# One small tile padded from 4 to 64 bytes, so that every weight tile lies 64 bytes further on in SBUF

## The chip, the cores and the metric

The kernel runs on one core of a Trainium2 chip. The metric is the device time of one execution in microseconds (us); less is better. Engines are named as the profile names them: PE is the matmul engine, PEld its weight load (the load of the stationary operand), DVE the vector engine, ACT the scalar engine, POOL and SP the two engines that here mostly issue DMAs.

## What is computed

Two layers of a hybrid decoder trunk, 512 tokens by 1024 features, float32. Cut to what matters:

```python
for l in range(2):
    h = rms_norm(x, gn[0])
    x = x + 0.5 * rms_norm(swiglu(h, w_ffn1_gate[l], w_ffn1_up[l], w_ffn1_down[l]), gn[1])
    h = rms_norm(x, gn[2])
    proj = h @ w_in[l]            # q, f, i, gate; attention q, k, v; two branch gates
    y_hg = hgrn2_mixer(...) @ w_branch_hgrn[l]
    y_at = swa_sink_attention(...) @ w_branch_attn[l]
    x = x + rms_norm((sigmoid(gate_a) * y_hg + sigmoid(gate_b) * y_at) @ w_out[l], gn[3])
    h = rms_norm(x, gn[4])
    x = x + 0.5 * rms_norm(swiglu(h, w_ffn2_gate[l], w_ffn2_up[l], w_ffn2_down[l]), gn[5])
```

The inner width of each SwiGLU is 2816. Nearly all arithmetic is in the products of activations with weights.

## The kernel before

Each float32 operand of a large product is split into a rounded part and a rest (`hi` and `lo`, type float32r), and a product is three matmuls: hi with hi, hi with lo, lo with hi (`mm3`, L411 to L415; every matmul is recorded at L114 in `mm`). Every matmul has its own weight load of 128x128, so PE and PEld each show 13571 instructions. A matmul is named by what it writes and reads: `acc<-s,whi` writes a PSUM tile `acc`, streams an activation tile `s` through the array and has a block of the weight tile `whi` as its stationary operand; in `acc<-whi,s` the weights stream and the activations are stationary.

The order of the matmuls is written out by hand; the other engines are scheduled around them. The SwiGLU's first half (`sevenths`, L1029, called from `fast`, L1064) is a seven-product scheme on halves of the tokens: its matmuls have 256 columns, and activations stream. The first blocks of each SwiGLU and the gates in the mixer stream 512 columns of activations (`wmm`, L417). The second half of each SwiGLU and the output projection (`down`, L699, with `piece` and `quarters`) and `project_tok` (L1016) stream 512 columns of weights over stationary activations.

Weights arrive through `Stream` (L156). `load` (L235) brings 128x1024 pieces from HBM into `w32` tiles (four slots) by DMAs on SP's queue; `split` (L322) turns each into `whi` and `wlo` (six slots each) on ACT, DVE and, for a part of them, by an accumulating DMA on POOL's queue (L360).

All SBUF tiles but the constants come from one pool, `sb`. A tag gets its slots when its first tile is asked for, one tag behind the other, and a slot's size is rounded up to 32 bytes. The first tag is `s` (`big`, L62: 61 slots of 2048 bytes, all activations), the second is `warm`, and behind it follow `w32`, `whi`, `wlo`, `tt`, `m` and the small tags. In the built program the slots of `s` start 64 bytes past a multiple of 512, and those of `w32`, `whi` and `wlo` 128 bytes past one. Blocks inside a tile are cut at multiples of 512 bytes (256-column halves at 1024), so that these two remainders hold for every large matmul's operands: counted within 512 bytes, weights lie 64 bytes, or 16 float32 numbers, behind activations.

The tile `warm` (L138) is 128x1, written once by ACT ahead of the first matmuls; nobody reads it. A second tile of the same tag is asked for in `down` (L821).

```python
def small(shape, tag, bufs=4, dt=F32):                                        # L65
    return sb.tile(shape, dt, tag=tag, name=nm(tag), bufs=bufs)
...
nc.scalar.activation(out=small([P, 1], "warm", 2), in_=eps_t, ...)            # L138
...
warm = small([P, 1], "warm", 2)                                               # L821
```

Of the kernel before, what the change touches and what calls it, by code (L numbers as in the profile page):

```python
# [10 lines left out]
AF = mybir.ActivationFunctionType  # L11
# [4 lines left out]
P = 128  # L16
# [28 lines left out]
def trunk(ctx: ExitStack, tc: tile.TileContext, xin, wall, gains, lbT, hgain, sinks, c_dist, c_mask, c_ident, out):  # L45
    nc = tc.nc
# [11 lines left out]
    def nm(s):  # L58
        seq[0] += 1
        return f"{s}_{seq[0]}"  # L60
# [4 lines left out]
    def small(shape, tag, bufs=4, dt=F32):  # L65
        return sb.tile(shape, dt, tag=tag, name=nm(tag), bufs=bufs)
# [7 lines left out]
    def const(shape, name, dt=F32):  # L74
        return cp.tile(shape, dt, tag=name, name=name)
# [59 lines left out]
    nc.vector.memset(ones, 1.0)  # L135
    eps_t = const([P, 1], "eps_t")
    nc.vector.memset(eps_t, EPS)
    nc.scalar.activation(out=small([P, 1], "warm", 2), in_=eps_t, func=AF.Copy, scale=eps_t)  # L138


    p = aux()
# [1503 lines left out]
```

## Time and profile before

| | us |
|---|---|
| median of 2 runs | 2068.94 |
| the two runs | 2067.01 and 2070.87 |
| the profiled execution | 2067.36 |
| its span, first to last instruction | 2064.8 |
| DVE busy | 1629.0 |
| ACT busy | 1249.3 |
| POOL busy | 268.0 |

The span is the time from the first to the last instruction of the profiled execution; the 2.6 us between it and that execution's time lie outside. "Busy" sums an engine's instructions, so that engines at work together are each counted in full. Starts of matmuls are recorded, their ends are modelled; the distance between two starts, called the pitch below, is therefore the better measure of PE's speed.

### The profile page before, as it was taken

How to read it: one execution, taken by the hardware profiler on the slowest of the kernel's cores; microseconds unless marked ns; L12 is line 12 of the kernel's file. 1: busy time of each engine (PE TensorE's matmuls, PEld its weight loads, DVE VectorE, ACT ScalarE, POOL GpSimd, SP SyncE). 2: the span in 40 equal slices, each digit the busy share in tenths (PEclk: the TensorE clock that was granted, in tenths of full speed). 3: DMA queues.
4: the chain of work that ended last, by engine and by line, in shares of the span. 5: the costliest groups of instructions: out<-in, count | busy, mean ns of one | idle time of the engine just before them, and what ended most of it. 6: DMA issues, size and time to landing. Idle time of an engine off the chain costs nothing. (4 is left out here: it accounts for less than half of the span.)

```text
span 2064.8 us, 36590 instructions
## 1 busy us (share of the span) xinstructions
PE 2053.1 (99%) x13571; PEld 1826.7 (88%) x13571; DVE 1629.0 (79%) x2910; ACT 1249.3 (61%) x2209; POOL 268.0 (13%) x318
## 2 busy tenths in 40 slices
PE   9999999999999999999999999999999999999999
PEld 8899978887888999997899998898778989999987
DVE  5887899666776778888988788977676758788888
ACT  7566687456355556658866666864653545666684
POOL 0111140000000011113201121400000100111140
PEclk9999999999999999999999999999999999999999
DMA  8587798312237367878758878872122562778794
GB/s 250 151 188 192 187 196 242 103 62 72 72 95 212 113 145 190 189 188 206 205 152 189 196 187 202 185 220 84 52 82 62 137 190 93 182 191 189 181 203 123
DMA packets 166802, 328.07 MB, mean 159 GB/s; under 512 B 19072, under 2 KB 85088, under 8 KB 166624
## 3 DMA queue, kind: packets, MB, share of 16 engines
q1 hardware_dynamic: 122416, 228.16, 33.1%
q0 software_dynamic: 44064, 97.54, 28.3%
q8 instruction: 106, 1.74, 0.3%
q14 instruction: 72, 0.59, 0.1%
q10 hardware_dynamic: 144, 0.05, 0.0%
HBM read 213.43 MB, written 14.73 MB: 110 GB/s over the span
## 5 line engine op out<-in xcount | busy, mean ns | idle before, releaser
L114 PE MATMUL acc<-s,whi 128*128 128x256 f32 (+1 forms) x4976 | 1031.0, 306 | 0.0
L114 PEld LDWEIGHTS acc<-s,whi 128*128 128x128 f32 x4976 | 793.8, 188 | 52.4 <-issue 3.2
L114 PE MATMUL acc<-s,wlo 128*128 128x256 f32 (+1 forms) x2488 | 759.9, 305 | 2.5 <-DMA wlo<-w 1.9
L114 PEld LDWEIGHTS acc<-s,wlo 128*128 128x128 f32 x2488 | 467.9, 188 | 30.7 <-DMA wlo<-w 4.4
L114 PE MATMUL acc<-whi,s 128*128 128x512 f32 x1360 | 446.6, 397 | 1.9 <-DVE s L432 1.3
L353 ACT CAST whi<-w 128x1024 fp32r<-128x1024 f32 (+1 forms) x310 | 286.8, 928 | 139.4 <-PE acc L114 90.0
L353 ACT CAST whi<-tt 128x1024 fp32r<-128x1024 f32 x160 | 167.9, 1049 | 252.3 <-DVE tt L347 171.4
L360 POOL DMA_DIRECT2D wlo<-w x178 | 154.2, 868 | 1249.5 <-ACT wlo L357 539.1
L114 PEld LDWEIGHTS acc<-whi,s 128*128 128x128 f32 x1360 | 255.7, 188 | 62.5 <-DVE s L432 2.2
L362 DVE TENSOR_TENSOR wlo<-tt,whi 128x1024 fp32r<-128x1024 f32 x160 | 196.0, 1225 | 135.7 <-ACT whi L353 129.8
L114 PE MATMUL acc<-wlo,s 128*128 128x512 f32 x680 | 267.6, 394 | 0.6 <-DVE wlo L294 0.6
L114 PE MATMUL aux<-s,whi 128*128 128x256 f32 (+1 forms) x1296 | 230.1, 280 | 0.0
L362 DVE TENSOR_TENSOR wlo<-w,whi 128x1024 fp32r<-128x1024 f32 (+1 forms) x132 | 157.5, 1204 | 78.7 <-ACT whi L353 77.8
L114 PEld LDWEIGHTS aux<-s,whi 128*128 128x128 f32 x1296 | 197.5, 188 | 1.1 <-issue 0.5
L114 PE MATMUL aux<-s,wlo 128*128 128x256 f32 (+1 forms) x648 | 181.0, 279 | 0.0
L114 PEld LDWEIGHTS acc<-wlo,s 128*128 128x128 f32 x680 | 128.0, 188 | 29.9 <-DVE wlo L294 2.4
L357 ACT ACTIVATE wlo<-w 128x1024 fp32r<-128x1024 f32 (+1 forms) x178 | 153.5, 863 | 0.2 <-PE acc L114 0.2
L114 PE MATMUL aux<-whi,s 128*128 128x512 f32 x432 | 145.3, 394 | 0.0
L443 POOL DMA_DIRECT2D s<-s x128 | 111.3, 969 | 217.5 <-ACT s L431 98.5
L114 PEld LDWEIGHTS aux<-s,wlo 128*128 128x128 f32 x648 | 121.6, 188 | 0.4
L294 DVE TENSOR_TENSOR wlo<-s,whi 128x512 fp32r<-128x512 f32 x160 | 102.5, 683 | 9.9 <-ACT whi L286 8.1
L431 ACT CAST s<-s 128x512 fp32r<-128x512 f32 (+1 forms) x140 | 70.6, 547 | 44.5 <-DVE s L490 41.0
(185 smaller groups left out, 2481.6 us busy)
## 6 DMA issues: line engine op xcount, KB each, us to landing
w<-wall SPq DMA_DIRECT2D x267, 512.0 KB, 4.1
wlo<-w POOLq DMA_DIRECT2D x98, 512.0 KB, 5.3
w<-wall SPq DMA_DIRECT2D x224, 128.0 KB, 3.5
wlo<-w POOLq DMA_DIRECT2D x80, 256.0 KB, 3.3
s<-wall SPq DMA_DIRECT2D x128, 128.0 KB, 4.4
s<-s POOLq DMA_DIRECT2D x64, 256.0 KB, 4.9
x_d<-s SPq DMA_DIRECT2D x48, 256.0 KB, 3.8
s<-x_d SPq DMA_DIRECT2D x48, 256.0 KB, 5.3
```

What stands on the lines that cost most here:

```text
L114: nc.tensor.matmul(o, lhsT, rhs, start=start, stop=stop)
L294: pin(nc.vector.tensor_tensor(it.lo[:, h[c]], w[c], it.hi[:, h[c]].bitcast(F32), op=ALU.subtract))
L353: i = nc.scalar.copy(it.hi[:, c], w[:, c])
L357: i = nc.scalar.mul(it.lo[:, c], w[:, c], -1.0)
L360: nc.gpsimd.dma_start(it.lo[:, c].bitcast(F32), w[:, c], accum_op=ALU.add)
L362: self.hold(nc.vector.tensor_tensor(it.lo[:, c], w[:, c], it.hi[:, c].bitcast(F32), op=ALU.subtract))
L431: (hold or ws.hold)(nc.scalar.copy(hi, src))
L443: nc.gpsimd.dma_start(lo.bitcast(F32), src, accum_op=ALU.add)
```

## The change

One tile's width, at L138:

```diff
-    nc.scalar.activation(out=small([P, 1], "warm", 2), in_=eps_t, func=AF.Copy, scale=eps_t)
+    nc.scalar.activation(out=small([P, 16], "warm", 2)[:, :1], in_=eps_t, func=AF.Copy, scale=eps_t)
```

The instruction writes the same single column. The tag's two slots grow from 32 to 64 bytes each, and everything that lies behind them in the pool moves by 64 bytes: `w32`, `whi`, `wlo`, `tt`, `m` and all small tags. The tiles of `s`, the constants and PSUM stay. Counted within 512 bytes, weights then lie 128 bytes behind activations where it was 64, and start 192 bytes past a multiple of 512. No instruction, wait or DMA is added, removed or reordered.

## The prediction, as put on record before the run

> **What bounds the kernel now.** I read the page's totals first, then the waits of PE, then the stretches of PE's own work.
>
> ```profile
> span 2064.8 us, 36590 instructions
> PE 2053.1 (99%) x13571; PEld 1826.7 (88%) x13571; DVE 1629.0 (79%) x2910; ACT 1249.3 (61%) x2209; POOL 268.0 (13%) x318
> PEclk9999999999999999999999999999999999999999
> ```
>
> PE is busy for 99% of the span at the full granted clock. The view of waits, for PE alone, shows how little stands still:
>
> ```profile
> PE acc L114 <- DMA wlo<-w: 1.9, 2, 1.2
> PE acc L114 <- DVE s L432: 1.3, 2, 0.7
> ...
> PE acc L114 <- DVE wlo L294: 0.6, 2, 0.3
> ```
>
> The largest wait sums to 1.9 us. So the time is the number of matmuls times their pitch, and an address can matter only through the pitch, or through work so much slower that PE starts to wait. The next view is that of stretches (time from and to, PE's busy time and matmuls, granted clock, DMA share, GB/s). The first four hold 256-column matmuls alone, the last two almost only 512-column ones with weights streaming:
>
> ```profile
> core 0: us, PE busy (x), PEclk, DMA share, GB/s
> 92.00:232.00 140.00, 140.00 (x1237) 1.00 0.80 190
> 740.00:910.00 170.00, 169.66 (x1466) 1.00 0.80 189
> 1120.00:1250.00 130.00, 128.76 (x1096) 1.00 0.81 191
> 1840.00:1930.00 90.00, 90.00 (x766) 1.00 0.80 189
> 950.00:1000.00 50.00, 49.69 (x217) 1.00 0.90 192
> 1265.00:1310.00 45.00, 45.00 (x194) 1.00 0.96 223
> ```
>
> The same work on the same sizes and at the same clock has two speeds: 140.00/1237 = 113.2 ns in layer 1's first SwiGLU, 128.76/1096 = 117.5 ns in layer 2's, 90.00/766 = 117.5 ns in its second, and 169.66/1466 = 115.7 ns, a mixture, between. The 512-column work shows 229.0 and 232.0 ns. In order of time the second pair is sharper (start, length, count):
>
> ```profile
> 63.74 0.63 PE L114 MATMUL acc<-s,whi 128*128 128x512 f32 x2
> ...
> 65.14 0.63 PE L114 MATMUL acc<-s,whi 128*128 128x512 f32 x2
> ```
> ```profile
> 960.23 0.62 PE L114 MATMUL acc<-whi,s 128*128 128x512 f32 x2
> ...
> 961.60 0.62 PE L114 MATMUL acc<-whi,s 128*128 128x512 f32 x2
> ```
> ```profile
> 1269.65 0.63 PE L114 MATMUL acc<-whi,s 128*128 128x512 f32 x2
> ...
> 1271.75 0.40 PE L114 MATMUL acc<-whi,s 128*128 128x512 f32 x1
> ```
>
> From 960.23 to 961.60 there are six matmuls, 228.3 ns each; from 1269.65 to 1271.75 nine, 233.3 ns each; with activations streaming, from 63.74 to 65.14 six, 233.3 ns each. None of them waits for a semaphore. I read this as two ways in which the streamed operand's reads and the next weight load's reads, which run at the same time, can fall into step; a stretch keeps one for tens of us. That the step has to do with addresses is my reading; the trace shows the two speeds, not their cause.
>
> **The change part by part.** *The write of `warm`*: one ACT instruction of the same one column, nothing. It runs ahead of the first matmul; were it slower, PE's start has other covers. Nothing.
>
> *The move of DVE's, ACT's and POOL's operands* by 64 bytes: no count changes. They are covered by PE's 99%; I take nothing, and the waits above are what would grow if I were wrong.
>
> *The move of the DMAs' targets.* The rows are
>
> ```profile
> w<-wall SPq DMA_DIRECT2D x267, 512.0 KB, 4.1
> wlo<-w POOLq DMA_DIRECT2D x98, 512.0 KB, 5.3
> ```
>
> A weight piece lands 4.1 us after its issue and four are under way, so a few tenths of a us more are covered. Uncovered, the dearest place is the stretch 1265 to 1310 with its DMA share of 0.96: if transfers there became 10% slower, up to 4.5 us would show in each such 45 us. I take nothing. The Trainium skill, "DMA: Bandwidth & Descriptors", section "How a descriptor splits into AXI transactions", says that a transfer not starting at a multiple of 256 bytes costs one more transaction; the tiles start 128 past one now and 192 past one then, so it changes neither the sum nor a chance.
>
> *The pitch* is the whole question. The groups by shape give the counts, and their mean lengths the share of the slow step:
>
> ```profile
> L114 PE MATMUL acc<-s,whi 128*128 128x256 f32 x3840 | 669.2, 278 | 0.0
> L114 PE MATMUL acc<-s,wlo 128*128 128x256 f32 x1920 | 535.5, 279 | 2.5 <-DMA wlo<-w 1.9
> L114 PE MATMUL acc<-whi,s 128*128 128x512 f32 x1360 | 446.6, 397 | 1.9 <-DVE s L432 1.3 <-ACT whi L286 0.6
> L114 PE MATMUL acc<-s,whi 128*128 128x512 f32 x1136 | 362.0, 400 | 0.0
> L114 PE MATMUL acc<-wlo,s 128*128 128x512 f32 x680 | 267.6, 394 | 0.6 <-DVE wlo L294 0.6
> L114 PE MATMUL aux<-s,whi 128*128 128x256 f32 x1280 | 224.6, 278 | 0.0
> L114 PE MATMUL acc<-s,wlo 128*128 128x512 f32 x568 | 224.3, 395 | 0.0
> L114 PE MATMUL aux<-s,wlo 128*128 128x256 f32 x640 | 177.8, 278 | 0.0
> L114 PE MATMUL aux<-whi,s 128*128 128x512 f32 x432 | 145.3, 394 | 0.0
> L114 PE MATMUL aux<-wlo,s 128*128 128x512 f32 x216 | 85.1, 394 | 0.6 <-DVE wlo L294 0.6
> ```
> ```profile
> L114 PE MATMUL acc<-s,whi 128*128 128x256 f32 x64 | 11.0, 276 | 0.0
> ```
> ```profile
> L114 PE MATMUL acc<-s,whi 128*128 128x256 f32 x66 | 11.8, 281 | 0.0
> ```
>
> The last two rows are that group in 180 to 196 us, a fast stretch, and in 1190 to 1206, a slow one. 256 columns: 3840+1920+1280+640 = 7680 matmuls; their mean length is 278.25 ns between 276 and 281, so 2.25/5 = 45% are slow, by 117.5-113.2 = 4.3 ns each. 512 columns: 1136+568 = 1704 with activations streaming, which I take as all slow (the one stretch quoted is), and 1360+680+432+216 = 2688 with weights streaming, which I take as half slow (one quoted stretch of each kind), by 233.3-228.3 = 5.0 ns.
>
> Bounds from these rows. All fast: 7680 x 0.45 x 4.3 = 14.9 us, 1704 x 5.0 = 8.5, 2688 x 0.5 x 5.0 = 6.7, together -30 us. All slow: 7680 x 0.55 x 4.3 = 18.2, and 6.7, together +25 us. What a distance of 128 bytes does is in no row, for the 64 holds for every large matmul. The nearest other distance is 0: attention's scores have both operands in `s`.
>
> ```profile
> 431.07 0.98 PE L114 MATMUL aux<-s,s 64*128 64x256 f32 x12
> ```
>
> Twelve matmuls of 256 columns on half the rows, which run in pairs: less the 0.28 us of a last matmul's length, 0.70/6 = 117 ns a pair, the slow step and no worse. At the distances 0, +64 (activations streaming) and -64 (weights streaming) I thus see the same two steps. So I take 128 to deal the steps out again in about the shares of now: a sum of 0, with -30 and +25 as its ends. The profiled execution took 2067.36 us (span 2064.8 and 2.6 around it), 1.6 under the runs' median; I forecast for the median, 2068.94 + 0, or **2069 us**.
>
> The Trainium skill speaks for no effect at all: "SBUF — State Buffer", section "Who interferes with whom", has PE wait on no one, and "TensorE: Matmul & The Clock Gate" (section "What happens when you issue a matmul") gives the moving operand and the weight load a read port each. By it the sum is 0 as well, but the two speeds above should not be there; no run here shows yet whether they come from the ports.
>
> **The rivals.**
> *A worse step (slower).* At 128 bytes the reads could meet more often, and a third step appear as far above the slow one as that is above the fast: 121.8 and 238.3 ns. Then all matmuls go slow (+25), and one step more, 7680 x 4.3 = 33 and 4392 x 5.0 = 22: +80, 2149 us. For it: one step exists that nothing else explains, and 128 is a rounder distance than 64. Against it: at distance 0, where I would expect the worst, no third step shows. It decides from +41 us, half of it.
>
> *A lower step (faster).* The same mirrored: all fast (-30) and one step below, -33 and -22: -85, 1984 us. Against it: no row here is under 113.2 ns. The Trainium skill ("TensorE: Matmul & The Clock Gate", "Back-to-back issue gap") has N/2.4 + 2.5 ns, 109.2 and 215.8. By that the sum would be near -113 us, an estimate from the page; this trace stays above it everywhere.
>
> *All fast, or all slow,* without a new step: 2039 and 2094 us, both within 2%.
>
> *DMA.* Weight loads slower by 10% and uncovered where the DMA share is 0.9 or more: about 4 such stretches of 45 us, +18 us, 2087. Against it: 1.9 us of DMA waits now.
>
> *The move does not happen*, because slots are rounded to more than 64 bytes or the tag is laid elsewhere: 2069 us.
>
> **How the numbers follow.** Steps dealt out as now, or no move: 0.30. All slow 0.10, all fast 0.08, DMA 0.03. Worse step 0.36, lower step 0.13. So faster by over 2% 0.13, within 2% 0.51, slower by over 2% 0.36; 2% is about what a measurement of this kernel can tell from no change. The likeliest case has its own range, 2039 to 2094. The range to hold it 8 times in 10 takes in the worse step and leaves out the lower one and what lies above 2150: 2036 to 2150.
>
> **What would show it.** Pitches in the same stretches: 92 to 232 us and 1120 to 1250 us at 113.2 or 117.5 ns confirm the two steps; 121 ns or more is the worse step, 109 the lower. If the stretches keep their present speeds one by one, the addresses do not matter. PE's waits should stay at some us; a DMA row at their head would be the DMA rival. The groups of DVE and ACT should keep their mean lengths. What makes me wrong most easily is that distance 0 in attention, on half the rows, is no fair sample of full matmuls.

## The result, and the profile after

The changed kernel takes 2087.15 us (two runs, 2086.83 and 2087.48) against 2068.94 before: ratio 1.0091, 95% interval 1.0073 to 1.0108. It is slower by 18 us, clear of the runs' scatter and under 2%. The forecast was 2069 us, the range 2036 to 2150.

The order of instructions on every engine is the same in both kernels, so the two profiles can be laid side by side. First the page of the changed kernel, its totals:

```profile
span 2085.4 us, 36590 instructions
## 1 busy us (share of the span) xinstructions
PE 2079.3 (100%) x13571; PEld 1854.6 (89%) x13571; DVE 1632.0 (78%) x2910; ACT 1251.8 (60%) x2209; POOL 267.5 (13%) x318
```

The span grew by 20.6 us, PE's busy time by 26.2. DVE and ACT grew by 3.0 and 2.5 us, POOL not at all: PE alone carries the time. What PE waits for, in the changed kernel (this is the whole answer):

```profile
PE aux L114 <- DVE eps_t L137: 1.1, 1, 1.1
PE acc L124 <- DVE s L862: 0.5, 1, 0.5
PE aux L114 <- DVE s L476: 0.3, 1, 0.3
```

The weight tiles, which headed the list before, are gone from it: a slower PE no longer runs into them. The stretches of the prediction, in the changed kernel (time, PE's busy time and matmuls, granted clock, DMA share, GB/s):

```profile
92.00:232.00 140.00, 140.00 (x1182) 1.00 0.81 190
1120.00:1250.00 130.00, 130.00 (x1098) 1.00 0.80 189
1840.00:1930.00 90.00, 90.00 (x761) 1.00 0.80 190
```

140.00/1182 = 118.4 ns, 130.00/1098 = 118.4, 90.00/761 = 118.3, where it was 113.2, 117.5 and 117.5. The clock is the same. The two speeds of before are gone, and one slow speed stands in all three stretches. Over all starts, only two calls in the mixers (168 of the 7680 matmuls of 256 columns) leave it, at 120.0 ns. In order of time, changed kernel (start, length, count):

```profile
1190.21 0.28 PE L114 MATMUL aux<-s,wlo 128*128 128x256 f32 x1
1190.33 0.40 PE L114 MATMUL aux<-s,whi 128*128 128x256 f32 x2
1190.56 0.28 PE L114 MATMUL aux<-s,wlo 128*128 128x256 f32 x1
1190.68 0.40 PE L114 MATMUL aux<-s,whi 128*128 128x256 f32 x2
1190.92 0.28 PE L114 MATMUL aux<-s,wlo 128*128 128x256 f32 x1
```

From 1190.21 to 1190.92 there are six matmuls in 0.71 us, and no wait among them.

All recorded starts of matmuls give the balance. Below, a pitch is the mean distance from a start of that kind to PE's next start, distances over 130 ns (256 columns) or 260 ns (512) set aside as gaps.

| kind (count) | pitch before, ns | pitch after, ns | all distances, us | of this gaps, us |
|---|---|---|---|---|
| 256 columns, activations streaming (7680) | 115.2 | 118.7 | 890.8 to 912.0 | 6.2 to 0.4 |
| 512 columns, activations streaming (1728) | 233.3 | 232.8 | 410.3 to 409.8 | 7.2 to 7.6 |
| 512 columns, weights streaming (2688) | 230.2 | 232.5 | 631.4 to 631.5 | 12.6 to 6.5 |

The column "gaps" counts what the distances set aside have beyond the pitch. The sum of the changes is 21.2 - 0.5 + 0.1 = 20.8 us; the span's is 20.6. The 256-column pitch costs 7680 x 3.5 = 27 us and the weights streaming 2688 x 2.3 = 6 us; some 12 us of gaps that PE had before are gone. PE's waits for semaphores, as their view sums them, are only 5 us of these 12 (6.9 before, 1.9 after): a short gap hides under a matmul's modelled length, 278 ns on average for 256 columns.

### The profile page after: what moved, and what is told of

It reads as the page before. It is cut to its first block, busy times and chain, and to the rows that moved or that the text cites. A ratio compares the mean times of both kernels' runs of the same rounds, so it can differ in the third digit from the quotient of the medians.

```text
span 2085.4 us, 36590 instructions
## 1 busy us (share of the span) xinstructions
PE 2079.3 (100%) x13571; PEld 1854.6 (89%) x13571; DVE 1632.0 (78%) x2910; ACT 1251.8 (60%) x2209; POOL 267.5 (13%) x318
## 4 chain that ended last, share of the span: by engine, by line
PE 98%; DMA 1%; DVE 0%; ACT 0%; issue 0%; SPq 0%; DVEq 0%; ACTq 0%
PE acc L114 74%; PE aux L114 22%; PE aux L124 2%; PE acc L124 0%; DMA s<-xin 0%; DMA w<-wall 0%; DVE s L462 0%; SPq L244 0%; DVE wlo L362 0%; ACT whi L353 0%; SPq L1493 0%; ACT s L531 0%; ACT L474 0%; DVE s L862 0%; ACT s L638 0%
## 5 line engine op out<-in xcount | busy, mean ns | idle before, releaser
L114 PE MATMUL acc<-s,whi 128*128 128x256 f32 (+1 forms) x4976 | 1049.2, 308 | 0.0
L362 DVE TENSOR_TENSOR wlo<-tt,whi 128x1024 fp32r<-128x1024 f32 x160 | 196.0, 1225 | 137.4 <-ACT whi L353 131.6
L114 PE MATMUL aux<-s,whi 128*128 128x256 f32 (+1 forms) x1296 | 236.9, 283 | 0.0
L286 ACT CAST whi<-s 128x512 fp32r<-128x512 f32 x160 | 90.3, 615 | 18.2 <-PE aux L114 12.0
```

Source lines behind the costliest of these rows:

```text
L114: nc.tensor.matmul(o, lhsT, rhs, start=start, stop=stop)
L286: i = nc.scalar.copy(it.hi[:, h[c]], w[c])
L362: self.hold(nc.vector.tensor_tensor(it.lo[:, c], w[:, c], it.hi[:, c].bitcast(F32), op=ALU.subtract))
```

## The experiments

My theory after the result: the distance between the stationary and the streamed operand in SBUF sets the pitch. Rivals: the weights' own place sets it; or any perturbation deals the two old speeds out anew. "Distance" is what the weights lie behind the activations, 64 in the kernel before and 128 in the changed one. Where only one run was taken, its time stands beside 13 runs of the kernel before: median 2069.01, from 2064.97 to 2072.07.

### All moved together

```diff
-    eps_t = const([P, 1], "eps_t")
+    eps_t = const([P, 24], "eps_t")[:, :1]
```

> Activations, weights and the small constants behind the first one all move by 64 bytes (one constant of 4 bytes is made 96 wide), so the weights start where they do in the changed kernel, 192 bytes past a multiple of 512, but lie 64 behind the activations as before. Theory, the distance between weights and activations decides: 256-column pitch a mixture of 113.3 and 117.8 ns as before, time within 0.4% of before, 2061 to 2077 us. Rival, the weights' own place decides: one pattern of 118.7 ns everywhere, about 2087. Rival, any perturbation deals the speeds out anew: the two old speeds in other shares, 2040 to 2094.

Measured: 2072.28 us (ratio 1.0018, interval 1.0007 to 1.0029). Two stretches of this kernel:

```profile
92.00:232.00 140.00, 140.00 (x1191) 1.00 0.81 189
1140.00:1240.00 100.00, 99.88 (x880) 1.00 0.80 191
```

140.00/1191 = 117.5 ns and 99.88/880 = 113.5 ns: the two old speeds are both back, though the weights start where they do in the changed kernel. Over all matmuls 115.5, 233.3 and 230.4 ns (in the order of the table above), as before. So the weights' own place is not it. But the stretches have changed roles: 92 to 232 us is slow here and was fast before. At one and the same distance something else picks between the two.

### The distance in steps of 64, and of 32

The two slots of the small tile become 6, 8 or 16 (distances 192, 256, 512), then 1 or 3 (32, 96), at both places that ask for it:

```diff
-    nc.scalar.activation(out=small([P, 1], "warm", 2), in_=eps_t, func=AF.Copy, scale=eps_t)
+    nc.scalar.activation(out=small([P, 1], "warm", 6), in_=eps_t, func=AF.Copy, scale=eps_t)
...
-        warm = small([P, 1], "warm", 2)
+        warm = small([P, 1], "warm", 6)
```

> Weights 192 bytes behind the activations (six slots of 32 bytes for the small tile in place of two). Distance theory: a third pattern, neither that of 64 nor that of 128; if what counts repeats every 128 bytes it is the pattern of 64 (2061 to 2077 us). Rival, own place of the weights counted in 128 bytes: here they start at a multiple of 128 as before, so as before, 2069. Rival of chance: the two old speeds in any shares, 2040 to 2094.

> Weights 256 bytes behind. Distance theory: again a pattern of its own, and that of 128 (118.7 ns everywhere, about 2087 us) if what counts repeats every 128 bytes. Rival of chance: the two old speeds in any shares, 2040 to 2094.

> Weights 512 bytes behind, so the remainders within 512 are the same as the activations'. Distance theory: attention's 117 ns at equal remainders suggests 117 to 118 ns everywhere, about 2085 us. Rival, repeats every 256 or 128 bytes: the same as at 256 or 128. Rival of chance: 2040 to 2094 with the two old speeds.

> Weights 32 bytes behind the activations (one slot of 32 bytes for the small tile). So far the pitches repeat every 256 bytes of distance: at 0 (and 256, 512) 120.0 ns for 256 columns, 227.7 and 226.8 ns for 512 (activations streaming, weights streaming); at 64 113.3 or 117.8, then 233.3 and 228.9 or 233.3. Theory, whole steps of 64 bytes count: 32 is one of these two, about 2076 or 2069 us. Rival, the distance counts byte by byte: pitches between the two, 114 to 119 ns, 228 to 231, about 2065.

> Weights 96 bytes behind. If whole steps of 64 bytes count, the pattern of 64 (113.3 or 117.8; 233.3; 228.9 or 233.3; about 2069 us) or of 128 (118.7; 232.8; 232.5; about 2087). If the distance counts byte by byte, between: 115 to 119 ns, about 2078.

| distance | 256 columns, ns | 512, activations streaming | 512, weights streaming | time, us |
|---|---|---|---|---|
| 64 (before) | 115.2: 113.3 or 117.8 | 233.3 | 230.2: 228.9 or 233.3 | 2068.94 |
| 128 (the change) | 118.7 | 232.8 | 232.5 | 2087.15 |
| 192 | 117.2: 113.3 or 117.8 | 229.3 | 233.3 | 2073.89 |
| 256 | 120.0 | 227.7 | 227.2 | 2074.72 |
| 512 | 120.0 | 227.7 | 227.2 | 2076.39 |
| 32 | 118.4 | 233.1 | 233.3 | 2086.41 |
| 96 | 118.6 | 234.1 | 233.3 | 2089.93 |

All but the first two times are single runs. At 192 a mostly fast and a slow stretch stand in one kernel, 140.00/1225 = 114.3 ns and 100.00/852 = 117.4:

```profile
92.00:232.00 140.00, 140.00 (x1225) 1.00 0.79 190
1140.00:1240.00 100.00, 100.00 (x852) 1.00 0.79 190
```

Rows for three more of these kernels, the stretches 92 to 232 us and 960 to 990 us; distance 256, then 512:

```profile
92.00:232.00 140.00, 140.00 (x1169) 1.00 0.80 189
960.00:990.00 30.00, 30.00 (x133) 1.00 0.90 192
```
```profile
92.00:232.00 140.00, 140.00 (x1169) 1.00 0.80 189
960.00:990.00 30.00, 30.00 (x134) 1.00 0.90 192
```

Distance 32:

```profile
92.00:232.00 140.00, 140.00 (x1185) 1.00 0.80 189
960.00:990.00 30.00, 30.00 (x130) 1.00 0.95 217
```

140.00/1169 = 119.8 ns and 140.00/1185 = 118.1 in the stretch of 256 columns; in that of weights streaming, 133 and 134 matmuls fit into the 30 us at distance 256 and 512 against 130 at 32. Distances 256 and 512 agree in every kind, and 128 differs from both: in these kernels the pattern repeats after 256 bytes and not after 128. The signs show too. What streams and what is loaded swap roles between the last two kinds, so a distance of 64 for the one is -64 for the other; and 192 is -64 when counted in 256. The table has just that mirror: 233.3 and 228.9 at 64, 229.3 and 233.3 at 192; and at 0 and 128, which are their own mirrors, the two 512-column kinds agree within 0.5 ns. Distance 0 (256, 512) is the worst for 256 columns and the best for 512, which is why its time hardly differs from before: 921.8 us in place of 890.8 for the 256-column kind, 618.2 and 400.9 in place of 631.4 and 410.3 for the others, together +8. Pitches of 120.0 and 227.2 ns are neither of the old speeds of their kind, so the rival that only deals these out anew falls.

At 192 I expected a third pattern; for 256 columns it is the two speeds of 64. My expectation for 512 had the direction for 256 columns and missed that 512 columns would gain. (The expectation for 32 quotes 226.8 ns for weights streaming at 0; over all starts it is 227.2.) At 32 and 96 both theories missed: neither is a copy of a neighbour, and the times, 2086 and 2090, do not lie between the neighbours' either. Half steps are no better than the whole ones here.

### Each matmul by its own two operands

If the two operands decide, each matmul can have its own distance. Weight tiles are made 64 numbers (256 bytes) wider, and each tile's data is put at the start (distance 64) or 48 numbers further on (256, that is 0):

```diff
-SLOTS = 61
+SLOTS = 60
...
-            it.hi = sb.tile([P, D], F32R, tag="whi", name=nm("whi"), bufs=WS)
-            it.lo = sb.tile([P, D], F32R, tag="wlo", name=nm("wlo"), bufs=WS)
+            z = 0 if it.kind in "abcd" else 48
+            it.hi = sb.tile([P, D + 64], F32R, tag="whi", name=nm("whi"), bufs=WS)[:, z : z + D]
+            it.lo = sb.tile([P, D + 64], F32R, tag="wlo", name=nm("wlo"), bufs=WS)[:, z : z + D]
```

> Two distances in one kernel: weight tiles are 256 bytes wider, and the blocks of the seven-product scheme lie 64 behind the activations as before, all others 0 behind (counted within 256). One activation slot fewer makes the room (60 for 61). Distance theory: the 512-column matmuls go to 227.7 and 226.8 ns, 1657 x 5.6 and 2304 x 3.4 ns less, -17 us; the first blocks of each SwiGLU and mixer, 960 of 256 columns, go to 120 ns, +3; the rest keeps its two speeds: about 2055 us. Rival, the pattern belongs to the kernel's whole layout and not to each matmul's two operands: no such split, 2069 to 2087.

The control has `z = 0` throughout:

> The control to the mixture: the same wider weight tiles and 60 slots, all blocks 64 bytes behind as before. Distance theory: the two old speeds, 2062 to 2080 us. If the slot taken away costs by itself, PE's waits show it, and the mixture's time has to be read against this one.

Measured: 2065.04 us for the mixture, 2070.66 for the control, one run each. The control lies within the scatter of the kernel before, so the slot taken away costs nothing that one run shows. The wider tiles also put every other slot 256 bytes further on, counted in 512, and the control's pitches are still those of 64: the period of 256 once more. The split is there: the mixture has 227.7 and 227.4 ns for the 512-column kinds, the control 233.3 and 230.0. Of the 14 us that were to come, some 4 came, in one run and within the scatter of the kernel before, because the 256-column kind was slow more often: 117.4 ns against 115.2 before, 12.3 us over all its distances. The control, at 116.3 ns, has 4.7 of these 12.3 us already. Another part is the 120 ns of 960 matmuls left at distance 0; they go back to 64 in the next kernel, which marks the first four tiles of those SwiGLUs and mixers and tests `it.u in self.near` as well:

```diff
-            z = 0 if it.kind in "abcd" else 48
+            z = 0 if it.kind in "abcd" or it.u in self.near else 48
```

> The mixture, with the first four weight tiles of each SwiGLU and mixer whose blocks meet 256 columns also left at 64 behind, so that all 256-column matmuls are at 64 and all 512-column ones at 0. Distance theory: 512 columns at 227.7 and 227.4 ns, 256 columns at the two old speeds in shares that cannot be told ahead: against before -17 us at the same shares, 2052, from 2038 (all fast) to 2070 (all slow). Rival, the 120 ns blocks were not the reason why the mixture won only 4 us: 2065.

Measured: 2061.99 us, ratio 0.9971 (0.9958 to 0.9984): 0.3% faster than the kernel before over 9 runs against 12, the interval clear of 1 and the gain far under 2%. The 512-column kinds are again at 227.7 and 227.4 ns, and the 256-column kind at 117.3: nearly everywhere slow, and 11.2 us over before. Bringing the 960 matmuls back to 64 thus gave 1.1 us and not the 3 that I had put on them; most of what the mixture lost it lost to the slow speed. In this kernel even the first stretch is slow, 140.00/1191 = 117.5 ns, as in the control, while 134 matmuls fit into the 30 us of weights streaming, as at distance 512:

```profile
92.00:232.00 140.00, 140.00 (x1191) 1.00 0.81 190
960.00:990.00 30.00, 30.00 (x134) 1.00 0.96 189
```

### What picks between the two speeds at 64

The trace of the kernel before already holds a clue. At 1126 us, after a long fast stretch, PE waits once for a weight tile, and goes on slow:

```profile
1125.68 0.28 PE L114 MATMUL aux<-s,wlo 128*128 128x256 f32 x1
...
1126.36 0.28 PE L114 MATMUL aux<-s,wlo 128*128 128x256 f32 x1
...
1128.10 0.39 PE L114 MATMUL acc<-s,wlo 128*128 128x256 f32 x1 [1.24 <-DMA wlo<-w]
...
1128.56 0.28 PE L114 MATMUL acc<-s,wlo 128*128 128x256 f32 x1
...
1129.27 0.28 PE L114 MATMUL acc<-s,wlo 128*128 128x256 f32 x1
```

Six matmuls take 0.68 us before the wait and 0.71 after it, on the same kind of operands. In that trace, inside the long runs of the seven-product scheme, the speed changes within 1.5 us of such a gap, with one exception, at 841 us; other gaps change nothing. So I broke the sequence at the head of each of the 80 calls:

```diff
-        p1, p26, p57, p43 = acc()[:, :H2], acc(), acc(), aux()
+        p1, p26, p57, p43 = acc(), acc(), acc(), aux()
+        mm(p1[:64, H2 : H2 + 64], ones[:, :64], ones[:, :64], True, True)
+        p1 = p1[:, :H2]
```

> The kernel before, with one small matmul (64 columns on constants, into a part of a PSUM tile that nobody reads) at the head of each of the 80 calls of the seven-product scheme. It adds work of about 0.1 us a call, 8 us. Theory, which of the two speeds a stretch of 256-column matmuls takes is dealt anew when the even sequence of matmuls is broken: the changes of speed now fall on the heads of calls, and the long stretches of before (all fast from 92 to 232 us, all slow from 1129 to 1250 us) no longer stand as they were. Rival, the speed belongs to the operands of that stretch, such as their slots: 92 to 232 stays at 113.3 ns and 1129 to 1250 at 117.8. Time 2060 to 2100 us by either.

Measured: 2111.81 us (one run, beside 12 of the kernel before with a median of 2067.16), above the 2100 that I gave. The same stretches of this kernel, the added matmuls (two in the trace for each) among the counts:

```profile
92.00:232.00 140.00, 140.00 (x1167) 1.00 0.78 180
735.00:900.00 165.00, 165.00 (x1328) 1.00 0.72 168
```

The stretch from 92 us on, all fast before, is slow in each of its calls, and so are the SwiGLUs' other calls of the scheme, 117.8 ns in all 72; only the eight calls in the mixers stay fast, at 113.5. The rival, that a stretch's operands own its speed, falls. "Dealt anew" was not right either: the same break gave the same speed each time in the SwiGLUs. Within this kernel the speed follows the place in the sequence, not chance at each call. The sequence alone does not fix it: the kernel with all moved together has the sequence and the distance of the kernel before, and its stretches changed roles. The break also cost more than I said: of the 45.2 us in the span, 2.0 ns more pitch on 7680 and on 2688 matmuls is 21 us, and the other 24 us are 0.3 us a call where I had 0.1. That is net of 6 us of gaps in the weights-streaming kind that are gone (12.6 before, 6.5 here), so that a break costs nearer 0.4 us. Both edits together:

> Both edits together. Theory: as the mixture with all 256-column matmuls at 64, plus up to 8 us for the added matmuls, with the shares of fast and slow as the nudges deal them: 2046 to 2078 us. If the nudges happen to deal fast each time, 2046.

Measured: 2096.48 us, ratio 1.0131 (1.0106 to 1.0157), with 117.8 ns in all 256-column runs: slow throughout; the upper end that I gave, 2078, counted 8 us for the breaks, while the time is 34 us above the mixture without them, 4 of it by the pitch.

The last try hands the scheme over from 512-column matmuls at distance 64, as in the kernel before:

```diff
+                    ws.near.add(ws.n - 1)
                     ws.gates()
+                    ws.near.add(ws.n - 1)
...
+                ws.near.add(ws.n - 1)
                 ws.pairs(FT - p)
```

> The last mixture, and the one weight tile just ahead of each run of the seven-product scheme also left at 64 behind, though its matmuls have 512 columns (some 450 matmuls more at 64, +2.5 us). Theory, a run of 256-column matmuls takes the speed that the sequence before it hands over: entered from 512 columns at distance 64, as in the kernel before, the runs in layers 1 and 2 begin at 113.3 ns again and stay so until the first wait of PE, where the last mixture had 117.8 from the start; 256-column mean back from 117.3 to between 114.5 and 116.5 ns, time 2046 to 2058 us. Rival, the speed at the entry is not handed over by the distance ahead of it: mean 117 ns or more, 2062 to 2066 us.

Measured: 2063.01 us, ratio 0.998 (0.997 to 0.9989); 256 columns at 117.2 ns, slow from each entry on. The theory of the handover falls in this form: one tile's matmuls at distance 64 ahead of the run do not bring the fast speed back.

The recorded starts of these kernels show one thing more. The eight calls in the mixers have 113.4 or 113.5 ns, each of them, in the four kernels whose 512-column matmuls all lie at 64: before, all moved, the control, and the one with the added matmuls. They have 117.8 ns, each of them, in the four whose 512-column matmuls lie at 0, the last with a few put back to 64. The calls' own distance is 64 in all eight kernels, and the control and the second mixture differ in nothing but where the 512-column weights lie. So the distance of the 512-column work does bear on the speed at which these calls start; how it does is not shown.

## Why the prediction was right, and where not

*PE bounds the kernel, and only the pitch can move it.* Right, but for the gaps: the three kinds' distances, pitch and gaps together, grew by 20.8 us where the span grew by 20.6.

*Nothing for the write, for DVE, ACT, POOL and the DMAs.* Right: their rows stand within 3 us of before, PE's waits shrank, and the 512 KB loads land in 4.2 us after 4.1.

*Two steps of the pitch, tied to addresses.* I had called the tie my reading. The distances show it: the same instructions have 113.3 to 120.0 ns and 227.2 to 234.1 ns, by the distance and, at 64 and 192 above all, by which of two speeds a run is on.

*"I take 128 to deal the steps out again in about the shares of now: a sum of 0, with -30 and +25 as its ends."* This is the term that was mis-sized. The 256-column pitch went from 115.2 to 118.7, +27 us, with weights streaming +6, and shorter gaps gave 12 back: +20.6 in the span, +18 in the medians. The sum lies near my upper end, but not by the way that the end stood for. The two steps are not a stock from which any distance is served: at 128 no stretch was fast, and 118.4 ns stood in the stretches where I had named only 113.2 or 117.5, 109, and 121 or more. My bounds also left out the gaps, which shrink when PE slows. The pitches alone cost 33 us, more than the +25 of "all slow"; that the sum came out inside 2039 to 2094 by 12 us of vanished gaps, which I had not counted, is luck.

*The shares.* I took half of the weights-streaming matmuls as slow, by 5.0 ns each. The mean of 230.2 ns between 228.9 and 233.3 makes it 30%, by 4.4 ns; that changes the bounds by some 3 us at most.

*The attention rows as a sample of distance 0.* My 117 ns divided 0.70 us by six pairs, where six pairs have five distances. By the recorded starts the first is 228 ns and the other four 116.5 on average, so that the figure stands by luck. Full matmuls at 0 have 120.0 for 256 columns, and the best pitch of all for 512. Half-row matmuls in pairs were no fair sample, as the last sentence of the prediction feared. The step up to 120.0 is beyond the slow one, if not by as much as the worse-step rival had it (121.8), and it comes with a gain elsewhere.

*The rivals.* In time the DMA rival, 2087, is the measured one, by chance: no DMA stands among PE's waits, and the loads land 0.1 us later. "All slow", 2094, came nearest in mechanism, with 118.7 ns for its 117.5. The worse step did not come at 128, nor the lower one: the three kinds had 118.7, 232.8 and 232.5 ns. At 0 the 512-column pitch did go lower, to 227.2 ns; for 256 columns no stretch of any kernel went under 113.2. The N/2.4 + 2.5 ns that I set beside the lower step was no fair forecast: the Trainium skill ("TensorE: Matmul & The Clock Gate", "Back-to-back issue gap") gives it for an isolated matmul, and these are streams with a weight load for every matmul. The Trainium skill's rule that PE waits on no one ("SBUF — State Buffer", section "Who interferes with whom"), and its separate read ports for the two operands ("TensorE: Matmul & The Clock Gate", "What happens when you issue a matmul"), would have every distance the same; the measured 113.3 to 120.0 ns at one clock disagree.

*Open.* Which part of the memory the two reads meet in was not seen; that they meet at all is inferred from the period of 256 bytes and the mirror. What puts a run of 256-column matmuls at distance 64 on the fast or slow speed at its start is not settled: a wait, an added matmul or a move of all tiles together can change it, and in the mixers it went with the distance of the 512-column matmuls; the one tile ahead did not decide it. Whether the scatter of the kernel before (7 us over 13 runs, against 0.65 between the two runs of the changed one) comes from that was not tried. It would fit that the three last mixtures, slow nearly throughout, scatter by 2.9 us (9 runs), 1.4 (4 runs) and 3.6 (9 runs), but only one execution of each kernel was profiled.

## What to carry to other kernels

If PE is busy all the time, divide a stretch's time by its matmuls before looking for a cause elsewhere: in this kernel two speeds for one shape at one clock came from where the operands lay and from what ran before, and PE's waits, 6.9 us in all, do not account for them. Here the distance of the stationary from the streamed operand, counted within 256 bytes, was worth up to 6% of a matmul's pitch, with different best values for 256 and 512 columns, and giving each shape its own made the kernel 0.3% faster. A padding chosen for one shape should be measured on all of them, and a gain in pitch only counts as far as the producers can keep up: here the gaps between PE's starts were 26.0 us in the faster kernel and 14.5 in the slower.

## What was unexpected in the hardware

The best distance depends on the matmul's width: of those tried, 0 is worst at 256 columns (120.0 ns) and best at 512 (227.2 and 227.7). At distances 64 and 192 the same code has two stable speeds, 113.3 and 117.8 ns. It held one for over 100 us, and in the kernel before all changes but one inside a long run came right behind a gap.
